# Delta rule exponents as matmul sums, triangular inverses from 16x16 blocks, and two buffer moves

## The chip, the cores and the metric

One NeuronCore of one Trainium2 chip runs the whole program. The metric is the device time of one execution in microseconds, the median of several runs; lower is better. TensorE (PE), VectorE (DVE), ScalarE (ACT), GpSimd (POOL) and the DMA queues (SP and POOL issue) work side by side and meet at semaphores.

## The reference, cut to what matters

A hybrid block (input projection, then Hyena, gated linear attention "GLA" and a gated delta rule "GDN" side by side, output projection, MLP) is followed by two layers of windowed attention with an mLSTM. The change touches the GDN and the attention:

```python
def gdn_chunk_scan(q, k, v, g, beta, s0):      # 4 heads of 96, two directions
        gcum = jnp.cumsum(gc, axis=-1)
        diff = gcum[..., :, None] - gcum[..., None, :]
        kb = kc * bc[..., None]
        a = -jnp.einsum('bhid,bhjd->bhij', kb, kc) * jnp.exp(jnp.where(strict, diff, -jnp.inf))
        rhs = jnp.concatenate([kb * jnp.exp(gcum)[..., None], vc * bc[..., None]], axis=-1)
        sol = lax.linalg.triangular_solve(eye - a, rhs, left_side=True, lower=True, unit_diagonal=True)
        ...
        attn = jnp.einsum('bhid,bhjd->bhij', qc, kc) * jnp.exp(jnp.where(incl, diff, -jnp.inf))
        o = (qc * jnp.exp(gcum)[..., None]) @ s + attn @ v_new
```

q and k are normalised per head (`l2norm`). In attention each block of 128 queries ends with `out / den`, times a gate.

## The kernel before, in words

All data are float32; large products use the fp32r form with a high and a low part (`mm3`: three matmuls). The kernel works in chunks of 128 tokens, 10 chunks (2 of context, 8 of the sequence), 4 heads and 2 directions, so 80 triangles of 128x128.

**Gates** (`gdn_gates`, `gdn_qrow`): rows of 40 (head, chunk) pairs by 128 tokens hold cumulated log decays G, logs of the write gate and of the norms (`gdn_lnorm`, which loads three partial sums into a small tile `gnsq`). The sums that the exponents need per column are stored to DRAM (`gdnRA`, `gdnRG`) and read back broadcast over 128 partitions (`bcast_row`, L1069).

**gdn_U** (L1073 to L1095): for each head and direction a broadcast row `ra` (128x1280) is loaded; for each of the 10 chunks one DVE scalar_tensor_tensor adds the column term `nG` and takes the minimum with a mask; one ACT exponential over 1280 columns; then k times k from TensorE is multiplied in, and the result U goes to DRAM (`gdnU`).

**gdn_inv** (L1097 to L1127): for each pair of heads, the 32x32 diagonal blocks of U (80 blocks per direction, one per partition) come back from DRAM and are inverted by 31 steps of a multiply (L1120) and an add (L1121) each; direction 0 on DVE, direction 1 on POOL. The inverses and their transposes (an ACT copy, `iU<-iE`) are stored as `gdnEd` and `gdnDd`.

**gdn_E** (L1129 to L1173), one call per head and direction: U, the diagonal blocks E and their transposes D0 are loaded; off-diagonal 32x32 and then 64x64 blocks are made with two small matmuls each, out of PSUM tiles that rotate through three banks (`px`). The caller `gdn_pre` (L1183) then makes W and G from E and stores them. Its second part has its own memory pool, opened after that of gdn_U and gdn_inv is closed; tiles E (one per direction), the rows and G have one buffer each.

**gdn_scan** (L1231, lanes from L1243): two lanes of two heads each. A head begins with loads, exponents (`rg` broadcast, eight DVE operations on `at`, ACT exponentials of `at` and `qs`), then ten serial steps.

Beside these, `hy_mix` (Hyena's transform in DVE, PE, POOL and DMA work) and the remaining input projections (`pm` matmuls) are written next to them in the program. **What sets the order:** a planner of the framework, which simulates times, orders every engine's queue; data, buffers and PSUM banks bound it. Only PE in `attention` has an order by hand (`manual_schedule`). DVE, ACT, POOL and the SP and POOL DMA queues execute in order.

**attention** (L2302, called at L2263): per block of 8 heads, scores, softmax and values; `finish` (L2374 on) copies 1/den into a tile `r` on POOL (L2383), transposes it on PE into a `po` bank, loads the gate `gz` (L2389), multiplies the two on DVE (L2390) and the product with y on POOL (L2391). `r` shares the one buffer of the tag `fr` with the rope and silu scratch of the projection units that fill PE (`units`, L2220 to L2231, recorded as L263 and L293). `gz` has two buffers.

Of the kernel before, what the change touches and what calls it, by code (L numbers as in the profile page):

```python
# [96 lines left out]
def pack_consts1():  # L97
    P = Packer()
    j, i = np.meshgrid(np.arange(128), np.arange(128), indexing="ij")
    for nm, ok in (("gF", j <= i), ("gB", j >= i), ("gFs", j < i), ("gBs", j > i)):  # L100
        P.add(nm, np.where(ok, -NEG, NEG))
    return P
# [59 lines left out]
class Builder:  # L162
# [83 lines left out]
    def ps(self, tag="px"):  # L246
        return self.pools[tag].tile([128, 512], F32, name=self.nm(tag), tag=tag)
# [729 lines left out]
    def gdn_lnorm(self, sq, out):  # L977

        nc, V = self.nc, self.nc.vector
        t = self.small([40, 3, 128], "gnsq", 1)  # L980
        for i in range(3):
            nc.sync.dma_start(out=t[:, i], in_=sq[i].rearrange("h (c t) -> (h c) t", t=128))
        V.tensor_add(out=out, in0=t[:, 0], in1=t[:, 1])
        V.tensor_add(out=out, in0=out, in1=t[:, 2])
        self.act(out, out, AF.Ln, bias=self.epsc[:40])
        self.ts(out, out, -0.5, ALU.mult)

    def gdn_qrow(self, gt, sq):

        nc = self.nc  # L990
        lq = self.small([40, 128], "gnlq", 1)
        self.gdn_lnorm(sq, lq)
        self.ts(lq, lq, math.log(96 ** -0.5), ALU.add)
        gt["rg"] = self.dram("gdnRG", [2, 40, 128])
        for d in range(2):
            self.nc.vector.tensor_add(out=gt["G"][:, d], in0=gt["G"][:, d], in1=lq)
            nc.gpsimd.dma_start(out=gt["rg"][d], in_=gt["G"][:, d])

    def gdn_gates(self, tl, gd, sk):


        nc, V = self.nc, self.nc.vector
        R = tl("ac", 2, (128, 10, 128))
        aa, bb, g, lb = (R[:40, 2 * i : 2 * i + 2, :] for i in range(4))
        G, lk = self.small([40, 2, 128], "gnG", 1), self.small([40, 128], "gnlk", 1)
        self.gdn_lnorm(sk, lk)
# [18 lines left out]
        out = {}  # L1025
        p = self.ps()
# [7 lines left out]
        p = self.ps()  # L1034
# [14 lines left out]
        ra = self.dram("gdnRA", [2, 40, 128])  # L1049
        for d in range(2):  # L1050
            nc.gpsimd.dma_start(out=ra[d], in_=lb[:, d, :])
# [15 lines left out]
        return dict(G=G, ra=ra, nG=nG, beta=beta, nbg=nbg, el=el, ek=ek)  # L1067

    def bcast_row(self, t, src, h, c0=0):  # L1069
        v = src[h * 10 + c0 : h * 10 + 10, :].rearrange("c t -> (c t)").unsqueeze(0).broadcast_to([t.shape[0], TT - c0 * 128])  # L1070
        self.nc.sync.dma_start(out=t, in_=v)
# [25 lines left out]
    def gdn_inv(self, hp, tl, Ud, Ed, Dd):  # L1097

        nc = self.nc
        UE = []  # L1100
        for d in range(2):
            U, E = tl(f"iU{d}", 2, (80, 32, 32)), tl(f"iE{d}", 2, (80, 32, 32))
            for hh in range(2):
                for b in range(4):
                    bs = slice(b * 32, b * 32 + 32)
                    p0 = hh * 40 + b * 10
                    nc.sync.dma_start(out=U[p0 : p0 + 10], in_=Ud[hp * 2 + hh, d, :, bs, bs])
            nc.gpsimd.memset(E, 0.0)
            nc.gpsimd.memset(E.rearrange("p a b -> p (a b)")[:, ::33], 1.0)
            UE.append((U, E))  # L1110
        for i in range(31):
            for d in range(2):
                eng = nc.gpsimd if d else nc.vector
                U, E = UE[d]
                m = i if d else 31 - i
                rows = slice(0, m) if d == 0 else slice(m + 1, 32)
                cols = slice(m, 32) if d == 0 else slice(0, m + 1)
                nr, ncl = rows.stop - rows.start, cols.stop - cols.start
                t = tl(f"it{d}", 1, (80, 272))[:, : nr * ncl].rearrange("p (a b) -> p a b", b=ncl)
                eng.tensor_mul(out=t, in0=U[:, rows, m : m + 1].broadcast_to([80, nr, ncl]), in1=E[:, m : m + 1, cols].broadcast_to([80, nr, ncl]))  # L1120
                eng.tensor_add(out=E[:, rows, cols], in0=E[:, rows, cols], in1=t)  # L1121
        for d in range(2):
            U, E = UE[d]
            self.act(U, E.rearrange("p a b -> p b a"), AF.Copy)
            for hh in range(2):
                nc.gpsimd.dma_start(out=Ed[hp * 2 + hh, d].rearrange("b c j i -> (b c) j i"), in_=E[hh * 40 : hh * 40 + 40])
                nc.gpsimd.dma_start(out=Dd[hp * 2 + hh, d].rearrange("b c j i -> (b c) j i"), in_=U[hh * 40 : hh * 40 + 40])  # L1127

    def gdn_E(self, h, d, tl, ps, Ud, Ed, Dd, E, D1):  # L1129

        nc, V = self.nc, self.nc.vector
# [7 lines left out]
        v32 = lambda p: p[:, :320].rearrange("p (c t) -> p c t", t=32)  # L1139
# [43 lines left out]
    def gdn_pre(self, dr, gt):  # L1183
# [3 lines left out]
        Ud, Ed, Dd = (self.dr_gdn[n] for n in ("U", "E", "D"))  # L1187
        with ExitStack() as es:
            tl = self.tiler(self.pool(es, "gdnp"))
            for hp in range(2):  # L1190
                for h in (2 * hp, 2 * hp + 1):
                    kT = tl("k", 1, (96, TT))
                    nc.sync.dma_start(out=kT, in_=dr["k"][h * 96 : h * 96 + 96])
                    self.gdn_U(h, kT, gt, tl, self.ps, Ud)
                self.gdn_inv(hp, tl, Ud, Ed, Dd)
        with ExitStack() as es:
# [3 lines left out]
            for t in Es + D1:  # L1200
                nc.gpsimd.memset(t, 0.0)
            for h in range(4):
# [6 lines left out]
                for d in range(2):  # L1209
# [5 lines left out]
                    self.gdn_E(h, d, tl, self.ps, Ud, Ed, Dd, E, D1[d])  # L1215
# [27 lines left out]
    def gdn_lane(self, tl, dr, gt, orows, heads):  # L1243
# [6 lines left out]
        for h in heads:  # L1250
# [432 lines left out]
    def block1(self, x3, ey):  # L1683
# [349 lines left out]
    def layer2(self, l, md, xT, ex, x_in, x_out):  # L2033
# [21 lines left out]
        with ed, ExitStack() as eu:  # L2055
# [157 lines left out]
            with self.psums(po=1, pm=1), ExitStack() as e2:  # L2213
# [49 lines left out]
                self.attention(lambda tag, *k: ol("fr", *k) if tag == "r" else al(tag, *k), pa, order, kA, kB, vr, qd, saz, yT, sink, nsink, step, more)  # L2263
# [38 lines left out]
    def attention(self, al, pa, tiles, kA, kB, vr, qd, saz, yT, sink, nsink, step, more):  # L2302
# [71 lines left out]
        def finish(b):  # L2374
# [7 lines left out]
            r = al("r", 1, (128, 8, 64))  # L2382
# [77 lines left out]
```

## Time and profile before

| | us |
|---|---|
| median of 3 runs | 3780.87 |
| the runs | 3768.03 to 3788.92 |
| the profiled execution | 3778.99 |
| its span, first to last instruction | 3777.2 |
| PE busy in it | 3311.5 |
| DVE busy | 2444.6 |
| mean granted TensorE clock | 0.903 of full speed |

Times of rows are counted from the span's start. "Busy" is the union of an engine's instructions; matmuls overlap each other, so a matmul's own duration is longer than its share of PE. The chain of waits is followed back from the last instruction, and so is one path, not all of them.

### The profile page before, as it was taken

Reading aid. Unit: us, or ns where it says so; the run is one execution under the profiler, and the core shown is the slowest. Engines: PE = TensorE matmul, PEld = TensorE weight load, DVE = VectorE, ACT = ScalarE, POOL = GpSimd, SP = SyncE. Lnnn points to the kernel's source line nnn. Section 1 sums busy time; section 2 is a strip of 40 time slices with the busy share of each in tenths; the row PEclk is TensorE's granted clock in tenths of the full one; section 3 lists DMA queues with packets and bytes.
Section 4 is the critical chain, followed back from the end, with each engine's and each line's share of the span. In section 5 each row is a group of like instructions: output and inputs, shape, how many; then the busy total and the mean of one; then the engine's idle time right before and its main releaser. Section 6 shows DMA issues by size and latency. Waiting matters only on the chain.

```text
span 3777.2 us, 50749 instructions
## 1 busy us (share of the span) xinstructions
PE 3311.5 (88%) x18398; PEld 2757.2 (73%) x18398; DVE 2444.6 (65%) x4678; ACT 1553.7 (41%) x2979; POOL 1436.9 (38%) x1250
## 2 busy tenths in 40 slices
PE   6899869866787999999999799998699999998897
PEld 5568647755676777887788588887588778876785
DVE  8797772789666465555644757665567656665676
ACT  4453236433233342222212444443455554453662
POOL 3234695563555344333312201112535511113454
PEclk9799989677657899999999799999899999999998
DMA  7545627865413453222221111113424421124343
GB/s 257 179 143 176 170 65 191 269 193 160 120 51 120 168 174 92 76 84 78 75 81 45 62 50 55 50 55 100 143 87 134 151 64 58 54 69 131 109 134 134
DMA packets 363077, 435.22 MB, mean 115 GB/s; under 512 B 68891, under 2 KB 284163, under 8 KB 362828
## 3 DMA queue, kind: packets, MB, share of 16 engines
q1 hardware_dynamic: 335596, 334.35, 30.2%
q0 software_dynamic: 27232, 97.63, 7.1%
q8 instruction: 146, 2.39, 0.3%
q14 instruction: 103, 0.84, 0.1%
HBM read 330.09 MB, written 101.81 MB: 114 GB/s over the span
## 4 chain that ended last, share of the span: by engine, by line
PE 52%; DVE 16%; DMA 7%; issue 5%; ACT 5%; POOL 5%; SPq 0%; POOLq 0%; DVEq 0%; ACTq 0%
PE pm L251 30%; PE px L251 16%; PE pa L251 2%; PE px L260 1%; POOL iE L1121 1%; PE po L251 1%; PE pa L260 1%; DMA mr<-in_w_ada 1%; DVE ma L266 1%; DVE at L266 1%; ACT e L263 1%; DMA wr<-in_w_in 1%; POOL ma L386 1%; DVE wl L282 1%; DMA st<-gdnRG 1%
## 5 line engine op out<-in xcount | busy, mean ns | idle before, releaser
L251 PE MATMUL pm<-x,wh 128*128 128x512 f32 (+3 forms) x4768 | 1429.5, 381 | 1.8 <-DVE x L282 1.8
L251 PEld LDWEIGHTS pm<-x,wh 128*128 128x128 f32 (+2 forms) x4768 | 870.6, 190 | 166.5 <-issue 7.1
L251 PE MATMUL pm<-x,wl 128*128 128x512 f32 (+3 forms) x2384 | 912.7, 383 | 29.3 <-ACT u L263 18.1
L251 PEld LDWEIGHTS pm<-x,wl 128*128 128x128 f32 (+2 forms) x2384 | 454.3, 191 | 116.6 <-ACT u L263 20.5
L251 PE MATMUL pm<-wo,ch 128*128 128x512 f32 x832 | 273.6, 409 | 0.0
L282 DVE TENSOR_TENSOR wl<-wr,wh 128x1024 fp32r<-128x1024 f32 (+1 forms) x110 | 148.4, 1349 | 151.9 <-ACT wh L263 151.7
L1626 DVE TENSOR_TENSOR oa<-px,oa 128x512 f32<-128x512 f32 x240 | 161.7, 688 | 129.7 <-PE px L251 129.6
L386 POOL TENSOR_TENSOR ma<-ma,mr 128x1024 f32<-128x1024 f32 x63 | 160.1, 2542 | 172.1 <-ACT mr L263 152.0
L263 ACT ACTIVATE u<-pm 128x512 f32<-128x512 f32 (+2 forms) x204 | 108.3, 544 | 269.1 <-PE pm L251 236.3
L251 PE MATMUL px<-w2h,ml 128*128 128x512 f32 x480 | 194.6, 405 | 21.1 <-DVE ml L282 17.5
L251 PE MATMUL px<-w2h,mh 128*128 128x512 f32 x480 | 192.8, 402 | 0.0
L251 PE MATMUL px<-w2l,mh 128*128 128x512 f32 x480 | 192.1, 400 | 0.0
L251 PEld LDWEIGHTS pm<-wo,ch 128*128 128x128 f32 x832 | 163.9, 198 | 33.8 <-issue 0.4
L270 POOL TENSOR_SCALAR mkw<-kr,gws 128x128 f32<-128x128 f32 x144 | 80.6, 564 | 282.1 <-PE px L251 238.9
L251 PE MATMUL pm<-wo,cl 128*128 128x512 f32 x416 | 174.0, 418 | 7.2 <-POOL cl L282 6.2
L2344 DVE TENSOR_REDUCE amx<-pa 128x1 f32<-128x640 f32 (+2 forms) x144 | 107.5, 746 | 78.4 <-PE pa L251 77.3
L263 ACT ACTIVATE e<-e 128x1280 f32<-128x1280 f32 (+3 forms) x126 | 134.2, 1068 | 45.5 <-DVE e L270 42.5
L263 ACT ACTIVATE wh<-wr 128x1024 fp32r<-128x1024 f32 (+2 forms) x138 | 143.3, 1038 | 19.7 <-PE pm L251 12.5
L263 ACT ACTIVATE P<-pa,amx 128x640 f32<-128x640 f32 (+2 forms) x144 | 105.6, 734 | 104.0 <-DVE amx L270 90.4
L263 ACT ACTIVATE w2h<-wr 128x1024 fp32r<-128x1024 f32 x32 | 33.9, 1059 | 264.5 <-PE px L251 226.5
L1524 POOL TENSOR_TENSOR xr<-or,xr 128x512 f32<-128x512 f32 x72 | 93.8, 1303 | 105.0 <-DVE or L1523 89.6
L263 ACT ACTIVATE mr<-mr,silu_cc 128x1024 f32<-128x1024 f32 x63 | 72.3, 1148 | 141.8 <-DVE ma L266 127.0
(879 smaller groups left out, 7442.3 us busy)
## 6 DMA issues: line engine op xcount, KB each, us to landing
wr<-in_w_in SPq DMA_DIRECT2D x102, 512.0 KB
wr<-in_w_mlp SPq DMA_DIRECT2D x64, 512.0 KB
mr<-in_w_ada SPq DMA_DIRECT2D x48, 512.0 KB
TF<-dft SPq DMA_DIRECT2D x54, 384.0 KB
mr<-in_w_mod SPq DMA_DIRECT2D x32, 512.0 KB
xp<-xr POOLq DMA_DIRECT2D x26, 512.0 KB, 3.9
xr<-xp SPq DMA_DIRECT2D x26, 512.0 KB
wr<-in_w_out SPq DMA_DIRECT2D x24, 512.0 KB
```

The source lines that it names most:

```text
L251: self.nc.tensor.matmul(out, a, b, start=start, stop=stop)
L260: self.nc.tensor.transpose(out, in_, self.ident[:p, :p])
L263: self.nc.scalar.activation(out, in_, f, **kw)
L266: self.nc.vector.scalar_tensor_tensor(out=out, in0=in0, scalar=scalar, in1=in1, op0=op0, op1=op1)
L270: (eng or self.nc.vector).tensor_scalar(out=out, in0=in0, scalar1=s1, scalar2=s2, op0=op0, **kw)
L282: (leng or self.nc.vector).tensor_sub(out=lo, in0=src, in1=hi.bitcast(F32))
L386: nc.gpsimd.tensor_add(out=acc[v], in0=acc[v], in1=raw)
L1121: eng.tensor_add(out=E[:, rows, cols], in0=E[:, rows, cols], in1=t)
L1524: nc.gpsimd.tensor_add(out=xr[:, fs], in0=r, in1=xr[:, fs])
L1626: V.tensor_add(out=oa[t][:, fs], in0=p, in1=oa[t][:, fs])
L2344: V.reduce_max(m_, s[:, w0:768], axis=AX.X)
```

## The change

Exponents: the masks with -inf, a selector and the row and column terms become fp32r operands (high part in partitions 0 to 39, low part in 64 to 103), and TensorE adds mask, column term and row term into one PSUM bank, from which ACT takes the exponential. The loads of `ra` and `rg` and the DVE additions go. Inverses: DVE and POOL invert 16x16 blocks for both heads of a pair in one instruction (15 steps in place of 31); gdn_E makes the 32x32 inverses with two more products, and their transposes with DVE. Partial sums of norms land in a part of a tile `ac` (for k) or a smaller `gnsq`. In attention `r` is taken from the tag of `gz`.

```diff
+    def gdn_hilo(self, name, src):
+        t = self.small([128, 128], name, 1, F32R)
+        self.nc.gpsimd.memset(t.bitcast(F32), 0.0)
+        self.act(t[0:40], src, AF.Copy)
+        self.nc.vector.tensor_sub(out=t[64:104], in0=src, in1=t[0:40].bitcast(F32))
+        return t
...
+    def gdn_decay(self, p, gt, row, d, h, c0, n, mask):
+        pv, hc = p[:, : n * 128].rearrange("p (c t) -> p c t", t=128), h * 10 + c0
+        self.mm(pv, self.identR, mask[:, d * 128 : d * 128 + 128].unsqueeze(1).broadcast_to([128, n, 128]), True, False)
+        self.mm(pv, gt["ng"][d], self.gm[:, 256 + hc : 256 + hc + n].unsqueeze(2).broadcast_to([128, n, 128]), False, False)
+        for i in range(n):
+            self.gdn_row(pv[:, i], gt[row][d], hc + i, False, i == n - 1)
+
+    def gdn_row(self, p, row, hc, first, last):
+        self.mm(p, self.gm[:, 256 + hc : 257 + hc].broadcast_to([128, p.shape[0]]), row, first, last)
...
     def gdn_U(self, h, kT, gt, tl, ps, Ud):
-        for d in range(2):
-            ra, U = tl("ra", 2, (128, TT)), tl("U", 2, (128, 10, 128))
-            self.bcast_row(ra, gt["ra"][d], h)
-            for c in range(10):
-                col = d * 40 + h * 10 + c
-                self.stt(U[:, c], ra[:, c * 128 : c * 128 + 128], gt["nG"][:, col : col + 1], self.k["gFs" if d == 0 else "gBs"], ALU.add, ALU.min)
-            self.act(U, U, AF.Exp)
...
         for c0 in range(0, 10, 4):
             n = min(4, 10 - c0)
+            for d, U in enumerate(Us):
+                p = ps()
+                self.gdn_decay(p, gt, "ra", d, h, c0, n, self.gm)
+                self.act(U[:, c0 : c0 + n], C3(p, n), AF.Exp)
...
-    def gdn_inv(self, hp, tl, Ud, Ed, Dd):
+    def gdn_inv(self, hp, tl, Ud, Ed):
...
-            U, E = tl(f"iU{d}", 2, (80, 32, 32)), tl(f"iE{d}", 2, (80, 32, 32))
+            U, E = tl(f"iU{d}", 2, (80, 2, 16, 16)), tl(f"iE{d}", 2, (80, 2, 16, 16))
             for hh in range(2):
-                for b in range(4):
...
+                for b in range(8):
+                    bs = slice(b * 16, b * 16 + 16)
+                    nc.sync.dma_start(out=U[b * 10 : b * 10 + 10, hh], in_=Ud[hp * 2 + hh, d, :, bs, bs])
...
-        for i in range(31):
+        for i in range(15):
...
-            self.act(U, E.rearrange("p a b -> p b a"), AF.Copy)
...
-    def gdn_E(self, h, d, tl, ps, Ud, Ed, Dd, E, D1):
+    def gdn_E(self, h, d, tl, ps, Ud, Ed, E, D1, Ec):
...
+        for b in range(8):
+            nc.sync.dma_start(out=Ec[b * 16 : b * 16 + 16, :, b % 2 * 16 : b % 2 * 16 + 16], in_=Ed[h, d, b].rearrange("c j i -> j c i"))
+        D16, Zc, E32, D0 = (tl(n, 2, (128, 10, 32)) for n in ("D0", "Z", "Z", "D0"))
+        V.transpose(flat(D16), flat(Ec))
+        pz, pe = v32(ps()), v32(ps())
+        for c in range(10):
+            for b in range(4):
+                self.mm(pz[blk(b), c], U[blk(b), c, blk(b)], D16[blk(b), c])
+        V.tensor_mul(out=Zc, in0=pz, in1=self.k["dF" if d == 0 else "dB"].unsqueeze(1).broadcast_to([128, 10, 32]))
+        for c in range(10):
+            for b in range(4):
+                self.mm(pe[blk(b), c], Zc[blk(b), c], Ec[blk(b), c])
+        V.tensor_add(out=E32, in0=pe, in1=Ec)
+        V.transpose(flat(D0), flat(E32))
         for b in range(4):
-            nc.sync.dma_start(out=E[blk(b), :, blk(b)], in_=Ed[h, d, b].rearrange("c j i -> j c i"))
-            nc.sync.dma_start(out=D0[blk(b)], in_=Dd[h, d, b].rearrange("c j i -> j c i"))
+            self.act(E[blk(b), :, blk(b)], E32[blk(b)], AF.Copy)
...
-                rg, a = tl("st", 2, (128, T)), tl("at", 4, (128, 8, 128))
-                self.bcast_row(rg, gt["rg"][d], h, 2)
-                for c in range(8):
...
-                self.act(a, a, AF.Exp)
-                q = tl("qs", 4, (96, T))
-                self.act(q, rg[:96], AF.Exp)
+                a, q = tl("at", 4, (128, 8, 128)), tl("qs", 4, (96, T))
+                for c0 in (0, 4):
+                    p = ps()
+                    self.gdn_decay(p, gt, "rg", d, h, 2 + c0, 4, self.wmask)
+                    self.act(a[:, c0 : c0 + 4], C3(p), AF.Exp)
+                    p = ps()
+                    for i in range(4):
+                        self.gdn_row(p[:96, i * 128 : i * 128 + 128], gt["rg"][d], h * 10 + 2 + c0 + i, True, True)
+                    self.act(q[:, c0 * 128 : c0 * 128 + 512], p[:96], AF.Exp)
...
-                self.attention(lambda tag, *k: ol("fr", *k) if tag == "r" else al(tag, *k), pa, order, kA, kB, vr, qd, saz, yT, sink, nsink, step, more)
+                self.attention(al, pa, order, kA, kB, vr, qd, saz, yT, sink, nsink, step, more)
...
-            r = al("r", 1, (128, 8, 64))
+            r = al("gz", 2, (128, 8, 64))
```

## Rows read from the trace of the kernel before

**Rows 1.** The page's head and its first part: span, PE busy (share) xinstructions.
```profile
span 3777.2 us, 50749 instructions
...
PE 3311.5 (88%) x18398; PEld 2757.2 (73%) x18398; DVE 2444.6 (65%) x4678; ACT 1553.7 (41%) x2979; POOL 1436.9 (38%) x1250
```
**Rows 2.** The page's fourth part, chain that ended last, by line.
```profile
PE pm L251 30%; PE px L251 16%; PE pa L251 2%; PE px L260 1%; POOL iE L1121 1%; PE po L251 1%; PE pa L260 1%; DMA mr<-in_w_ada 1%; DVE ma L266 1%; DVE at L266 1%; ACT e L263 1%; DMA wr<-in_w_in 1%; POOL ma L386 1%; DVE wl L282 1%; DMA st<-gdnRG 1%
```
**Rows 3.** Windows: length, busy PE, PEld, DVE, ACT, POOL; clock, DMA share, GB/s.
```profile
350.00:478.00 128.00, 112.90 (x545) 94.36 (x544) 90.31 (x182) 32.08 (x41) 72.71 (x93) 0.93 0.65 179
478.00:575.00 97.00, 65.43 (x266) 47.63 (x264) 65.61 (x102) 34.38 (x41) 86.98 (x90) 0.84 0.28 80
...
670.00:811.00 141.00, 116.21 (x1189) 107.56 (x1189) 111.23 (x142) 72.00 (x127) 79.02 (x44) 0.74 0.76 239
811.00:1000.00 189.00, 109.80 (x615) 99.19 (x615) 156.78 (x297) 51.06 (x86) 83.27 (x43) 0.66 0.56 166
1000.00:1150.00 150.00, 123.62 (x1043) 105.83 (x1044) 110.70 (x202) 54.44 (x143) 90.42 (x62) 0.57 0.20 54
```
**Rows 4.** Chain of waits, 350 to 575 us, shares by line.
```profile
by line: POOL iE L1121 21.3%; DMA gdnU<-U 8.8%; POOL it L1120 8.5%; DVE U L266 7.9%; issue 7.0%; DVE it L1120 5.2%; DVE iE L1121 4.7%; DVE wl L282 3.6%; DVE ac L266 3.4%; PE pm L251 3.3%; ACT iU L263 1.9%; DMA wr<-in_w_in 1.8%; SPq L1107 1.
```
**Rows 5.** Timelines of POOL, DVE and PE, 485 to 540 us: start, length, what, [idle before].
```profile
485.12 0.35 POOL L1121 TENSOR_TENSOR iE<-iE,it 80x87 f32<-80x87 f32 x1
...
495.61 23.36 POOL L1121 TENSOR_TENSOR iE<-iE,it 80x207 f32<-80x207 f32 x1
...
518.09 0.42 DVE L1121 TENSOR_TENSOR iE<-iE,it 80x255 f32<-80x255 f32 x1
...
536.89 3.58 PE L251 MATMUL px<-e,cols 128*4 128x512 f32 x4 [22.16 <-ACT e L263]
```
**Rows 6.** Windows of the inverse's tile iE alone: length, busy DVE, ACT, POOL.
```profile
350.00:478.00 128.00, 29.93 (x56) 1.62 (x1) 55.30 (x73) 0.93 0.65 179
478.00:575.00 97.00, 32.74 (x68) 6.88 (x4) 69.81 (x68) 0.84 0.28 80
```
**Rows 7.** Groups of DVE and ACT, 340 to 1110 us: busy us, mean ns | idle before.
```profile
L266 DVE SCALAR_TENSOR_TENSOR at<-st,gnnG,consts 128x128 f32<-128x128 f32 x64 | 44.0, 753 | 12.3 <-DMA st<-gdnRG 12.3
L266 DVE SCALAR_TENSOR_TENSOR U<-ra,gnnG,consts 128x128 f32<-128x128 f32 x80 | 25.3, 389 | 18.0 <-DMA gdnU<-U 10.8 <-issue 7.2
...
L1155 DVE COPY E<-px 32x320 f32<-32x320 f32 x16 | 7.8, 486 | 19.3 <-PE px L251 19.0
...
L263 ACT ACTIVATE iU<-iE 80x1024 f32<-80x1024 f32 x4 | 8.5, 2125 | 27.6 <-POOL iE L1121 22.7 <-DVE iE L1121 4.8
...
L263 ACT ACTIVATE D<-D 32x320 f32<-32x320 f32 x16 | 7.5, 468 | 9.9 <-DMA D<-gdnDd 9.5
```
**Rows 8.** Timelines of PE and ACT in gdn_E.
```profile
593.70 1.35 PE L251 MATMUL px<-D,U 32*32 32x32 f32 x40
...
676.63 0.57 ACT L263 ACTIVATE W<-px 128x480 f32<-128x480 f32 x1 [2.86 <-issue]
...
802.62 0.57 ACT L263 ACTIVATE W<-px 128x480 f32<-128x480 f32 x1 [4.10 <-PE px L251]
```
**Rows 9.** Groups of PE, 575 to 1110 us.
```profile
L251 PE MATMUL px<-E,nk 128*96 128x128 f32 x160 | 22.2, 291 | 0.7 <-ACT W L263 0.7
```
**Rows 10.** Timeline of PE: two first matmuls of a triple, one triple apart.
```profile
505.73 0.39 PE L251 MATMUL pm<-x,wl 128*128 128x512 f32 x1
...
506.41 0.39 PE L251 MATMUL pm<-x,wl 128*128 128x512 f32 x1
```
**Rows 11.** Chain of waits, 620 to 1110 us, shares by line.
```profile
by line: PE px L251 31.1%; DVE at L266 6.6%; issue 5.4%; DMA st<-gdnRG 4.3%; PE pm L251 3.8%; DVE EO L266 3.6%; DVE fl L282 2.5%; DVE Y L518 2.1%; DMA hx<-hy 1.8%; DVE P L266 1.7%; DVE S L266 1.7%; DMA G<-gdn_GT 1.6%; DVE b L820 1.6%; DVE l
```
**Rows 12.** Group of PE in attention; timeline of DVE around 2770 us.
```profile
L260 PE MATMUL po<-consts,fr 128*128 128x128 f32 x72 | 13.0, 311 | 40.5 <-POOL fr L2383 37.5 <-DVE y L2371 2.2 <-POOL wo L282 0.8
...
2757.97 0.20 DVE L2381 RECIPROCAL arden<-arden 128x8 f32<-128x8 f32 x1
...
2770.17 0.69 DVE L293 TENSOR_TENSOR or<-or,fr 128x512 f32<-128x512 f32 x1 [1.80 <-ACT fr L263]
```

More of the change, by code (lines that the diff above doesn't have):

```diff
@@ L99, in pack_consts1 @@
     j, i = np.meshgrid(np.arange(128), np.arange(128), indexing="ij")
-    for nm, ok in (("gF", j <= i), ("gB", j >= i), ("gFs", j < i), ("gBs", j > i)):
-        P.add(nm, np.where(ok, -NEG, NEG))
+    for nm, ok in (("sF", j < i), ("sB", j > i)):
+        P.add(nm, np.where(ok, 0.0, NEG))
+    p, q = np.meshgrid(np.arange(128), np.arange(40), indexing="ij")
+    P.add("sel", (p % 64 == q).astype(np.float32))
+    p, q = np.meshgrid(np.arange(128) % 32, np.arange(32), indexing="ij")
+    P.add("dF", ((p >= 16) & (q < 16)).astype(np.float32))
+    P.add("dB", ((p < 16) & (q >= 16)).astype(np.float32))
     return P
@@ L974, in head_norm_out, with gdn_lnorm @@
                 nc.gpsimd.dma_start(out=rows(yT, row0), in_=gt)
-    def gdn_lnorm(self, sq, out):
+    def gdn_lnorm(self, sq, out, t):
         nc, V = self.nc, self.nc.vector
[L980 to L984, printed above, removed]
+        for i, o in enumerate((t[:, 0], t[:, 1], out)):
+            nc.sync.dma_start(out=o, in_=sq[i].rearrange("h (c t) -> (h c) t", t=128))
+        V.tensor_add(out=t[:, 0], in0=t[:, 0], in1=t[:, 1])
+        V.tensor_add(out=out, in0=out, in1=t[:, 0])
         self.act(out, out, AF.Ln, bias=self.epsc[:40])
         self.ts(out, out, -0.5, ALU.mult)
+    def gdn_hilo(self, name, src):
[4 more added lines that the diff above has]
+        return t
     def gdn_qrow(self, gt, sq):
-        nc = self.nc
         lq = self.small([40, 128], "gnlq", 1)
-        self.gdn_lnorm(sq, lq)
+        self.gdn_lnorm(sq, lq, self.small([40, 2, 128], "gnsq", 1))
         self.ts(lq, lq, math.log(96 ** -0.5), ALU.add)
-        gt["rg"] = self.dram("gdnRG", [2, 40, 128])
+        gt["rg"] = []
         for d in range(2):
             self.nc.vector.tensor_add(out=gt["G"][:, d], in0=gt["G"][:, d], in1=lq)
-            nc.gpsimd.dma_start(out=gt["rg"][d], in_=gt["G"][:, d])
+            gt["rg"].append(self.gdn_hilo(f"gnra{d}", gt["G"][:, d]))
+    def gdn_decay(self, p, gt, row, d, h, c0, n, mask):
[6 more added lines that the diff above has]
+        self.mm(p, self.gm[:, 256 + hc : 257 + hc].broadcast_to([128, p.shape[0]]), row, first, last)
     def gdn_gates(self, tl, gd, sk):
@@ L1048, in gdn_gates @@
         V.tensor_add(out=lb, in0=lb, in1=lk.unsqueeze(1).broadcast_to([40, 2, 128]))
-        ra = self.dram("gdnRA", [2, 40, 128])
-        for d in range(2):
-            nc.gpsimd.dma_start(out=ra[d], in_=lb[:, d, :])
+        V.tensor_sub(out=g, in0=lk.unsqueeze(1).broadcast_to([40, 2, 128]), in1=G)
+        ra, ng = ([self.gdn_hilo(f"gn{n}{d}", t[:, d]) for d in range(2)] for n, t in (("ra", lb), ("ng", g)))
         p = self.ps()
@@ L1066, in gdn_gates @@
         self.stt(nbg, nbg, -1.0, beta, ALU.mult, ALU.mult)
[L1067 to L1071, printed above, removed]
+        return dict(G=G, ra=ra, ng=ng, beta=beta, nbg=nbg, el=el, ek=ek)
     def gdn_U(self, h, kT, gt, tl, ps, Ud):
         nc = self.nc
-        kk = []
-        Us = []
-        for d in range(2):
-            ra, U = tl("ra", 2, (128, TT)), tl("U", 2, (128, 10, 128))
-            self.bcast_row(ra, gt["ra"][d], h)
-            for c in range(10):
-                col = d * 40 + h * 10 + c
-                self.stt(U[:, c], ra[:, c * 128 : c * 128 + 128], gt["nG"][:, col : col + 1], self.k["gFs" if d == 0 else "gBs"], ALU.add, ALU.min)
-            self.act(U, U, AF.Exp)
-            Us.append(U)
+        Us = [tl("U", 2, (128, 10, 128)) for _ in range(2)]
+        C3 = lambda p, n: p[:, : n * 128].rearrange("p (c t) -> p c t", t=128)
         for c0 in range(0, 10, 4):
             n = min(4, 10 - c0)
+            for d, U in enumerate(Us):
+                p = ps()
+                self.gdn_decay(p, gt, "ra", d, h, c0, n, self.gm)
+                self.act(U[:, c0 : c0 + n], C3(p, n), AF.Exp)
             p = ps()
@@ L1114, in gdn_inv @@
                 U, E = UE[d]
[L1115 to L1117 removed]
+                m = i if d else 15 - i
+                rows = slice(0, m) if d == 0 else slice(m + 1, 16)
+                cols = slice(m, 16) if d == 0 else slice(0, m + 1)
                 nr, ncl = rows.stop - rows.start, cols.stop - cols.start
[L1119 removed]
@@ L1120, in gdn_inv @@
-                eng.tensor_mul(out=t, in0=U[:, rows, m : m + 1].broadcast_to([80, nr, ncl]), in1=E[:, m : m + 1, cols].broadcast_to([80, nr, ncl]))
-                eng.tensor_add(out=E[:, rows, cols], in0=E[:, rows, cols], in1=t)
+                t = tl(f"it{d}", 1, (80, 2, 72))[:, :, : nr * ncl].rearrange("p h (a b) -> p h a b", b=ncl)
+                shape = [80, 2, nr, ncl]
+                eng.tensor_mul(out=t, in0=U[:, :, rows, m : m + 1].broadcast_to(shape), in1=E[:, :, m : m + 1, cols].broadcast_to(shape))
@@ L1122, in gdn_inv @@
+                eng.tensor_add(out=E[:, :, rows, cols], in0=E[:, :, rows, cols], in1=t)
         for d in range(2):
-            U, E = UE[d]
-            self.act(U, E.rearrange("p a b -> p b a"), AF.Copy)
             for hh in range(2):
-                nc.gpsimd.dma_start(out=Ed[hp * 2 + hh, d].rearrange("b c j i -> (b c) j i"), in_=E[hh * 40 : hh * 40 + 40])
-                nc.gpsimd.dma_start(out=Dd[hp * 2 + hh, d].rearrange("b c j i -> (b c) j i"), in_=U[hh * 40 : hh * 40 + 40])
-    def gdn_E(self, h, d, tl, ps, Ud, Ed, Dd, E, D1):
+                nc.gpsimd.dma_start(out=Ed[hp * 2 + hh, d].rearrange("b c j i -> (b c) j i"), in_=UE[d][1][:, hh])
@@ L1186, in gdn_pre @@
         nc = self.nc
-        Ud, Ed, Dd = (self.dr_gdn[n] for n in ("U", "E", "D"))
+        Ud, Ed = (self.dr_gdn[n] for n in ("U", "E"))
         with ExitStack() as es:
@@ L1194, in gdn_pre @@
                     self.gdn_U(h, kT, gt, tl, self.ps, Ud)
-                self.gdn_inv(hp, tl, Ud, Ed, Dd)
+                self.gdn_inv(hp, tl, Ud, Ed)
         with ExitStack() as es:
@@ L1199, in gdn_pre @@
             D1 = [tl("D1", 2, (128, 10, 64)) for _ in range(2)]
-            for t in Es + D1:
+            Ec = [tl("Ec", 2, (128, 10, 32)) for _ in range(2)]
+            for t in Es + D1 + Ec:
                 nc.gpsimd.memset(t, 0.0)
@@ L1214, in gdn_pre @@
                     nc.gpsimd.tensor_mul(out=W, in0=rows[1], in1=f("beta"))
-                    self.gdn_E(h, d, tl, self.ps, Ud, Ed, Dd, E, D1[d])
+                    self.gdn_E(h, d, tl, self.ps, Ud, Ed, E, D1[d], Ec[d])
                     G = tl("G", 1, (96, 10, 128))
@@ L1703, in block1 @@
             self.load_consts(kp, "consts1")
+            self.gm = kp.tile([128, 296], F32R, name="gm", tag="gm", bufs=1)
+            o = self.offs["consts1"][0]
+            for c0, nm in ((0, "sF"), (128, "sB"), (256, "sel")):
+                V.tensor_copy(out=self.gm[:, c0 : c0 + o[nm][1]], in_=self.k[nm])
             egg = ExitStack()
```

19 lines of the change are left out of this document (7 added, 12 removed).

## The prediction

> **What bounds the kernel now.** The page's head first: PE is busy 3311.5 of 3777.2 us, so 466 us at most are to be had without making its work less [rows 1]. The chain of the whole page gives PE nearly half, but lines of this change stand on it too: POOL's inverse step, DVE's `at`, the DMA that brings `st` from `gdnRG` [rows 2]. Since a mean over 3777 us hides stages, I cut windows around the Delta rule. Between 350 and 575 us PE is busy 112.9 + 65.4 of 225 us, so 47 us are idle there; from 670 to 1150 its clock is 0.74, 0.66 and 0.57, against 0.93 before 478 [rows 3] and 0.903 for the whole program. This stretch waits on chains, not on an engine that is full. The rest of the program is PE's and the change hardly touches it, attention apart.
>
> The execution shown took 3778.99 us, 1.9 below the median of 3780.87. The sum below is made against 3779. About 0.5% (19 us) is what a measurement here can tell from no change: faster means under 3762, slower over 3800.
>
> **Part 1: gdn_U and gdn_inv, 350 to 575.** The chain of these 225 us gives POOL `iE` 21.3%, `it` 8.5, DVE `it` 5.2 and `iE` 4.7, ACT `iU` 1.9: 41.6%, 94 us in the inverse [rows 4]. On `iE` alone POOL is busy 55.3 + 69.8 = 125.1 us, DVE 62.7, ACT 8.5 [rows 6]. One of POOL's steps lasts 23.36 us where one half its size lasts 0.35, and ends 0.5 us after the last of DVE's inverse steps; it lay beside DVE's whole run [rows 5]. The cost follows the number of steps and the overlap with DVE more than the elements. 62 multiply and add steps per pair of heads and direction become 30, for both pairs 124 become 60, with about half the elements each. POOL: 60 x 0.35 = 21 us in place of 125; DVE: 60 x 0.28 (a little over half of 62.7/124) = 17 in place of 62.7; ACT's 8.5 us go. The second pair's inverse, which held 478 to 573, should end near 490, and gdn_E with its own pool opens there: 87 us earlier for this line of work. DVE also loses 25.3 us of additions for U with the 18.0 us that they waited [rows 7].
>
> That is not 87 us of program: between 478 and 575 PE does projections that must be done anyhow. They gain what PE idles, 47 us at most. And the change adds PE work: per head and direction of gdn_U two sums over the first and second four chunks and a short third, 32 matmuls of 512 columns at 227 ns (a triple takes 0.68 us [rows 10]) plus 16 of 256 at half that, 9.2 us, and 80 row matmuls of 128 columns at about 139 ns by the nearest group [rows 9], 11 us: 20 (14 to 24, by 60 to 190 ns for a row matmul). 47 - 20 - 7 for what stays idle gives **20 us** for the projections. On SP, `iU` takes 64 small loads in place of 32 and `Ec` 64 in place of the 64 of E and D; 16 broadcasts go. All are queued ahead of gdn_E's loads only; covered while projections fill PE, some 14 us if that cover goes.
>
> A rule on the 23-us step: the Trainium skill ("SBUF — State Buffer", section "Who interferes with whom") says that a DVE instruction with two SBUF inputs contends with a GpSimd read, and that whoever comes first blocks the other for its whole instruction. By that rule a block lasts one DVE instruction, so the 23 us would have another cause, which fewer steps need not remove, and the sum would be that of rival 5 below, 3744, not 3722. The row shows a stall over a whole run of DVE steps, which the page does not state.
>
> **Part 2: gdn_E, 577 to 811.** Five steps (head, direction) of W evacuation lie between 676.63 and 802.62: 25.2 us a step [rows 8]. They run in series because three `px` banks rotate in program order, so the next step's first product waits for the evacuation of the previous step's G. A step gains, on that series: 40 matmuls of 32x32 (1.35 us [rows 8]), DVE's masking (0.5, like its 32x320 copy at 486 ns [rows 7]), 40 more (1.35), an addition (0.5), a transpose (0.5), four ACT copies (4 x 468 ns [rows 7] = 1.9): 6.1 us. From above: PE at half clock +2.7, and each of three DVE visits queues behind Hyena's work, DVE being busy 111 of 141 us [rows 3], about 1.3 us each: 13 us. From below: 0, if the step overlaps its neighbour, for E and D loads cost 9.5 us of ACT's waiting before [rows 7] and become one load that can be early. I take 9, nearer to the rows that name the operations: 8 x 9 = **+72** (0 to +104) for this line.
>
> **Part 3: gdn_scan.** DVE's 64 additions are 44.0 us [rows 7], and on the chain from 620 to 1110 (490 us) `at` holds 6.6%, the DMA from `gdnRG` 4.3%: 32 + 21 = 53 us [rows 11]. In their place PE forms 16 sums: 32 matmuls of 512 columns at 227 ns, 7.3, and 128 row matmuls at 139 ns, 17.8 (60 to 190 ns: 15 to 32 in all); ACT takes 32 exponentials of 512 columns from PSUM in place of 16 long ones over as many elements, 18 us by the 0.57 us of W's 480-column evacuation [rows 8], and so no more than before. Of this I put 33 us on the path at this clock: **-20**.
>
> **How the parts meet.** Two lines end near 1100. The Delta rule's own: -87 + 72 - 20 = -35. Hyena's and the projections': -20 from PE's idle time, and DVE, busy 156.8 of 189 us from 811 to 1000 [rows 3], loses about 100 us over the stretch (25.3 + 44.0 + 45.7, less 8 x 1.9 added); chain shares of DVE's Hyena lines `EO`, `fl`, `Y` are 8.2% of 490 = 40 us [rows 11], of which I take 15: -35. Both lines say **-35**, and the later one decides.
>
> **Part 4: attention.** Before the 72 transposes of 1/den PE idles 40.5 us, 37.5 of it behind POOL's copy into `fr` [rows 12]. In the case I followed, den was ready at 2758.2, but `fr` was held by silu scratch until 2770.9, when DVE's product ended [rows 12]. With the tag of `gz` this hold goes; r then sits in one of its two buffers and gz always in the other, so gz's load waits for POOL's product of the block before, a block earlier, which leaves it time. What remains is POOL's own queue (weight splits written ahead). I take 0.6 of 37.5: **-22** (0 to -37).
>
> Edits at no cost: high/low splits, the moved `gnsq`, and the copies to `gm` run on 40 to 128 short partitions while PE is full of projections; without that cover a few us.
>
> **Sum:** 3779 - 35 - 22 = **3722**.
>
> **Rivals.**
> 1. *The clock comes back.* On PE's 31.1% of the chain, 152 us of `px` work [rows 11] run at a mean of 0.66 [rows 3]. PE gets some 45 us of new work and fewer gaps; at 0.80 those 152 us become 125: -27. With two thirds of attention's remainder (-10): **3685**. For: the clock falls just where PE waits most. Against: the serial step gets longer, not denser. The Trainium skill ("TensorE: Matmul & The Clock Gate", Part 1) has it that the throttle is released by activity, which speaks for this rival; that 350 to 478, with PE busy 88%, has 0.93 agrees.
> 2. *r stays late.* POOL's splits and not `fr` held four of five copies: attention gives 0, the rest as forecast: **3744**.
> 3. *Hidden anyway.* Hyena's DVE line decides both ends and the projections only shift: the stretch gives 0, attention a few us: **3775**. For: DVE 156.8 of 189 us. It is also where the time would be if the planner's new order gave nothing earlier. That the change does not do what it says (sums wrongly hidden behind old waits, say) ends here too.
> 4. *Slower: gdn_E's round trips.* The new products put four more visits of DVE and ACT between PE's, and each step is serial. ACT stood still 2.86 and 4.10 us ahead of W [rows 8]; if every new visit costs 3.5 us behind Hyena's queue beside the 6.1 of work, a step grows by 20 us, 160 in all. The Delta rule's line: -87 + 160 - 20 = +53, less attention 22: **3810**. It decides from 16 us a step on, (87 + 20 + 22) / 8. For: DVE is busy 111 of 141 us there. Against: its waits are shared with the projections' and Hyena's, which go on meanwhile.
>
> 5. *POOL's long step comes back.* One POOL step of 23 us stands once more beside DVE's run, in the second pair, whatever the number of steps: 22 of the 87 us are not had, the Delta rule's line gives -87 + 22 + 72 - 20 = -13 in place of -35: **3744**. Against: DVE's run, which it outlasted by 0.5 us [rows 5], falls to about a quarter. This is the case that the page on SBUF leaves open.
>
> **Numbers.** Forecast 0.42; rival 1 0.17; rival 2 0.08; rival 3 0.15; rival 4 0.13; rival 5 0.05. Forecast, 1, 2 and 5 are under 3762: faster 0.72; rival 3 same 0.15; rival 4 slower 0.13. The forecast's own range is 3690 to 3755 (gdn_E's step between 6 and 11 us, attention 0 to -37). The whole range, 3660 to 3800, takes in rivals 1 to 3 and 5 with their bounds and leaves out most of rival 4 and a few hundredths below.
>
> **What would show it.** Right: POOL's last inverse step near 490 and none over 5 us; the first E product near 500; W evacuations 33 to 36 us apart; no `at` on DVE and no `gdnRG` on the chain; idle before the `po` transposes under 18 us. Wrong: the steps of gdn_E over 41 us apart (rival 4); a clock over 0.75 from 811 to 1150 (rival 1); PE still behind L2383's copy for over 30 us (rival 2); the last scan step near 1100 as now with DVE busy over 80% before it (rival 3).

## The result, and the profile after

The changed kernel took 3727.65 us (median of 4 runs) against 3777.36 before (4 runs): 49.7 us less, ratio 0.9868, 95% interval 0.983 to 0.9906. The forecast was 3722. The total came out; where it came from did not. The profiled execution's span is 3722.1 us. The head of the page and the windows that answer to [rows 1, 3], then one window of the first attention layer:

```profile
span 3722.1 us, 53759 instructions
...
PE 3350.3 (90%) x19966; PEld 2797.4 (75%) x19966; DVE 2339.3 (63%) x4512; ACT 1563.9 (42%) x3045; POOL 1350.8 (36%) x1182
```

```profile
350.00:478.00 128.00, 126.99 (x680) 108.24 (x678) 58.62 (x108) 37.02 (x63) 44.76 (x83) 1.00 0.51 137
478.00:575.00 97.00, 93.36 (x839) 72.31 (x838) 49.83 (x56) 47.82 (x73) 40.74 (x45) 0.98 0.50 136
670.00:811.00 141.00, 99.90 (x1339) 89.48 (x1340) 104.90 (x142) 68.20 (x120) 82.76 (x41) 0.71 0.65 203
811.00:1000.00 189.00, 144.87 (x1182) 131.55 (x1181) 127.78 (x246) 59.99 (x121) 78.14 (x43) 0.73 0.44 124
1000.00:1150.00 150.00, 133.22 (x1165) 115.82 (x1164) 83.72 (x202) 54.09 (x142) 72.79 (x49) 0.61 0.19 51
...
2700.00:2800.00 100.00, 95.98 (x617) 85.13 (x616) 73.32 (x134) 70.14 (x138) 50.39 (x43) 1.00 0.42 122
```

The first two lines look like a success: PE is busy 220 of 225 us where it was busy 178, at a granted clock of 1.00 and 0.98. Whether that is time won is seen only from where the stages end. Three lines of instructions mark them: W's evacuations in gdn_E (first and last start), the scan's products with `at`, and those of `v` in the gated linear attention (GLA), which runs after Hyena and beside the scan. Before:

```profile
L263 ACT ACTIVATE W<-px x16: 550/572/573, 624.6 to 807.6; 128x480 f32<-128x480 f32 x16
...
L251 PE MATMUL px<-W,at x128: 275/421/526, 873.8 to 1096.8; 128*128 128x96 f32 x128
...
L251 PE MATMUL px<-v,at x64: 245/421/529, 1056.5 to 1270.1; 128*128 128x96 f32 x64
```

After:

```profile
L268 ACT ACTIVATE W<-px x16: 548/571/572, 552.0 to 854.9; 128x480 f32<-128x480 f32 x16
...
L256 PE MATMUL px<-W,at x128: 275/386/527, 900.0 to 1131.9; 128*128 128x96 f32 x128
...
L256 PE MATMUL px<-v,at x64: 248/421/529, 1039.6 to 1268.9; 128*128 128x96 f32 x64
```

gdn_E starts 72.6 us earlier and ends 47.3 later, for it takes 303 us in place of 183 (from the first of these evacuations to the last). The scan ends 35 us later, and the linear attention, with which this stretch closes, at the same place (1.2 us earlier). PE's busy time from 350 to 1300, first before, then after:

```profile
sum 950.00, PE 747.61 PEld 632.52 DVE 623.93 ACT 340.57 POOL 531.45; mean PE 149.52 PEld 126.50 DVE 124.79 ACT 68.11 POOL 106.29
```

```profile
sum 950.00, PE 801.86 PEld 685.88 DVE 529.76 ACT 354.42 POOL 448.89; mean PE 160.37 PEld 137.18 DVE 105.95 ACT 70.88 POOL 89.78
```

PE is busy 54 us more and the stretch ends at the same place, so the idle time that the change removed went to the work that it added. DVE's 94 and POOL's 83 us less bought nothing that shows at the end. The gain stands in attention; the group of the transposes of 1/den that answers to [rows 12], and then, in the timelines of DVE and POOL, one block's reciprocal and copy:

```profile
L265 PE MATMUL po<-consts,gz 128*128 128x128 f32 x72 | 10.9, 274 | 4.0 <-DVE y L2403 4.0
```

```profile
2727.40 0.20 DVE L2413 RECIPROCAL arden<-arden 128x8 f32<-128x8 f32 x1
...
2727.74 0.61 POOL L2415 COPY gz<-arden 128x512 f32<-128x512 f32 x1 [0.46 <-DVE arden L2413]
```

The copy comes 0.14 us behind the end of the reciprocal, and the 37.5 us of waiting are gone.

### The profile page after: what moved, and what is told of

It reads as the page before. It is cut to its first block, busy times and chain, and to the rows that moved or that the text cites. A ratio compares the mean times of both kernels' runs of the same rounds, so it can differ in the third digit from the quotient of the medians.

```text
span 3722.1 us, 53759 instructions
## 1 busy us (share of the span) xinstructions
PE 3350.3 (90%) x19966; PEld 2797.4 (75%) x19966; DVE 2339.3 (63%) x4512; ACT 1563.9 (42%) x3045; POOL 1350.8 (36%) x1182
## 4 chain that ended last, share of the span: by engine, by line
PE 47%; DVE 10%; issue 5%; DMA 4%; ACT 4%; POOL 3%; SPq 0%; POOLq 0%; ACTq 0%; DVEq 0%
PE pm L256 28%; PE px L256 13%; PE pa L256 2%; PE po L256 1%; PE px L265 1%; PE pa L265 1%; DMA mr<-in_w_ada 1%; DVE ma L271 1%; ACT e L268 1%; DVE amx L2376 1%; DVE e L287 1%; DVE x L287 1%; DMA wr<-qd 1%; POOL ma L391 0%; POOL cl L287 0%
```

## Experiments

**Each part alone.** The theory after the traces (A): r's place is the whole gain. The rival (B): the prediction's sum.

attn_only:

```diff
-self.attention(lambda tag, *k: ol("fr", *k) if tag == "r" else al(tag, *k), pa, ...
+self.attention(al, pa, ...
...
-            r = al("r", 1, (128, 8, 64))
+            r = al("gz", 2, (128, 8, 64))
```

> Only the last two edits (r takes the tag of gz), the Delta rule as before. Theory A (r's place is the whole gain, because every late copy of r delayed the whole block of attention and not only its transposes): 45 to 53 us faster, about 3728. Theory B (the prediction's sum: 22 from attention, 35 from the Delta rule): about 3755. PE's idle time before the po transposes goes from 37.5 us to about 0 in both.

no_attn undoes these two lines in the changed kernel.

> The whole change but r left in the scratch fr. Theory A: within 8 us of the kernel before, 3770 to 3780, with the Delta rule's scan still ending some 35 us later than before. Theory B: about 3742.

exp_only takes gdn_hilo, gdn_decay, gdn_row and their callers; gdn_inv, gdn_E and attention stay as before.

> Only the exponents summed by TensorE (and the move of the norms' scratch); inverses of 32x32 and r as before. Theory A, with gdn_E's longer steps named as what ate the gain: the Delta rule's scan ends 10 to 40 us earlier than before, the program 0 to 15 us faster, since the linear attention that ends the stretch is not on that chain. Theory B: 20 to 30 us faster.

inv_only takes gdn_inv, gdn_E and Ec alone.

> Only the 16x16 inverses. Theory A: gdn_E starts 60 to 80 us earlier, its eight steps take 36 to 44 us each in place of 25, the scan ends 20 to 50 us later; the program from 5 us faster to 15 us slower. Theory B: 87 earlier and 72 longer, 10 to 20 us faster. If POOL's long step comes back (rival 5), one POOL inverse step of over 10 us stands in the trace.

inv_attn is inv_only with the edit of attn_only.

> The 16x16 inverses and r's place, without the exponents by TensorE. By the sum of the runs of single parts (45 from attention, 6 from the inverses): 3728, as the whole change; the exponents then give nothing. If the exponents need the early inverses to pay (the whole change less this run): 3740 or more. If they only add PE work: 3715 or less, and this run beats both kernels.

| run | us | before, same chip | ratio, 95% interval |
|---|---|---|---|
| attn_only | 3734.74 | 3779.39 | 0.9885 (0.9862 to 0.9909) |
| no_attn | 3771.84 | 3779.39 | 0.9987 (0.9968 to 1.0006) |
| exp_only | 3786.65 | 3779.39 | 1.0025 (0.9999 to 1.005) |
| inv_only | 3773.82 | 3779.39 | 0.9989 (0.9968 to 1.0011) |
| inv_attn | 3722.66 | 3781.20 | 0.9859 (0.9829 to 0.989) |

The size in theory A holds: r's place gives 44.7 us, the rest 7.5 with an interval that takes in nothing. Its reason (that a late copy delayed the whole block) no run tried by itself. The exponents alone lean to slower, and without them the other two parts are as fast as the whole change: they give nothing that shows. The scan of exp_only ends nearly where it did (1100.3 against 1096.8), not 10 us earlier: that expectation missed. In inv_only it ends 25 us later with steps of 42 us, as expected, and POOL's longest step is 6.6 us. In no_attn it ends 28 us later, where 35 were expected.

**What held r.** r_dve changes the kernel before, r_own the changed one:

```diff
-            nc.gpsimd.tensor_copy(out=r, in_=den...)
+            V.tensor_copy(out=r, in_=den...)
...
-            r = al("gz", 2, (128, 8, 64))
+            r = al("r", 1, (128, 8, 64))
```

> The kernel before, with r copied by DVE and not by POOL, still into the scratch fr. If POOL's queue (weight splits written ahead) held r, this gives 20 us or more, 3755 or less. If the buffer fr held it, nothing: 3765 to 3790, and PE still waits 30 us or more ahead of the po transposes, now for DVE.

> The whole change, with r in a buffer of its own, so that gz keeps both of its buffers. If gz's lost buffer costs something it shows here as 5 us or more under the change; if gz's load is early enough with one, as the prediction has it, the program is within 8 us of the change, 3718 to 3735.

r_dve: 3768.08, ratio 0.998 (0.9964 to 0.9996). A block of DVE's timeline, and PE's group:

```profile
2726.26 0.69 DVE L293 TENSOR_TENSOR or<-or,fr 128x512 f32<-128x512 f32 x1 [1.36 <-ACT fr L263]
2726.99 0.43 DVE L2383 COPY fr<-arden 128x512 f32<-128x512 f32 x1
```

```profile
L260 PE MATMUL po<-consts,fr 128*128 128x128 f32 x72 | 13.4, 317 | 34.4 <-DVE fr L2383 31.8 <-DVE y L2371 2.0 <-DVE amx L270 0.6
```

On another engine the copy still follows the silu product that frees `fr`, by 0.04 us, though 1/den was ready at 2711.2 and DVE stood idle for 1.36 us ahead of the product; PE still waits 31.8. With buffers of its own (the change, r_own) the wait is gone: the buffer held r. By the medians r_dve was 11 us faster than the kernel before (by the ratio 8); PE's wait is 5.7 us shorter, which may be POOL's queue. r_own: 3729.45, ratio 0.9875 (0.9845 to 0.9905), as the change; gz's lost buffer costs nothing that shows.

**Why the Delta rule gave nothing that shows.** Five kernels change gdn_E's new work inside the whole change. e_none leaves out what joins the 16x16 inverses:

```diff
...
-        V.tensor_mul(out=Zc, in0=pz, in1=...)
...
-        V.tensor_add(out=E32, in0=pe, in1=Ec)
-        V.transpose(flat(D0), flat(E32))
+        E32, D0 = Ec, D16
```

> The whole change, but gdn_E leaves out what joins the 16x16 inverses into 32x32 ones: both products, the mask, the addition and the second transpose (the off-diagonal 16x16 blocks stay zero). Theory A1 (the stretched steps of gdn_E push the scan into the linear attention and slow that down, so they ate the gain): steps about 25 us apart, the scan ends 60 to 110 us earlier than with the change, the program 15 to 30 us faster than it, 3695 to 3710. Theory A2 (Hyena and the linear attention end this stretch whatever the Delta rule does): the scan ends as much earlier, the program within 8 us of the change, 3718 to 3735.

e_act:

```diff
+        self.act(Zc[:, :, q0 : q0 + 16], pz[:, :, q0 : q0 + 16], AF.Copy, scale=self.k["dF" if d == 0 else "dB"][:, q0 : q0 + 1])
...
+            self.mm(pe[blk(b)], self.ident[blk(b), blk(b)], Ec[blk(b)], True, False)
...
+            self.mm(pd[blk(b)], self.ident[blk(b), blk(b)], D16[blk(b)], True, False)
...
+                self.mm(pd[blk(b), c], Ec[blk(b), c], Zc[blk(b), c], False, c == 9)
...
+        self.act(D0, pd, AF.Copy)
```

> The whole change, with the new visits of DVE in gdn_E replaced: ACT masks by a scale per partition, PE adds the diagonal blocks by an identity product and forms the transposes by products of its own, ACT evacuates. Only the first transpose stays on DVE. If DVE's queue behind Hyena's work is what stretches a step (theory A1): steps 28 to 33 us apart in place of 43, and the program 8 to 25 us faster than the change, 3703 to 3720. If the number of round trips stretches it, whichever engine serves them: 38 us or more and no gain.

e_dve:

```diff
-        V.tensor_mul(out=Zc, in0=pz, in1=...)
+        V.tensor_mul(out=Zc, in0=Ec, in1=...)
...
-        V.tensor_add(out=E32, in0=pe, in1=Ec)
+        V.tensor_add(out=E32, in0=Zc, in1=Ec)
```

> The whole change, with the two new products of gdn_E left out (the mask is applied to the 16x16 inverses themselves, and what comes of it is not the inverse), while the mask, the addition and the second transpose stay on DVE. It splits the 38 us by which the kernel without any of these beat the change. If the new visits in DVE's queue cost them: 3715 to 3735, as the change. If PE's two products and their round trips cost them: 3685 to 3700, as the kernel without. In between it splits by the number.

e_par has e_act's mask, `pd` as plain products, and

```diff
+        V.tensor_add(out=D0, in0=pd, in1=D16)
         V.tensor_add(out=E32, in0=pe, in1=Ec)
-        V.transpose(flat(D0), flat(E32))
```

> The whole change, computing the same with fewer visits in series: ACT masks by a scale per partition, the transposes come from 40 more small products on PE, and the two DVE additions stand side by side, so that DVE is on the series twice in place of four times. If DVE's visits cost the 38 us: 8 to 25 us faster than the change, 3703 to 3720. If PE's work does: the same or up to 15 us slower, 3725 to 3745.

e_thin:

```diff
-        for c in range(10):
+        for c in range(2):
...
+        V.tensor_mul(out=Zc[:, 2:], in0=Ec[:, 2:], in1=...)
...
+        V.tensor_add(out=E32[:, 2:], in0=Zc[:, 2:], in1=Ec[:, 2:])
```

> The whole change, with gdn_E's two new products made for two of the ten chunks only (16 small matmuls in place of 80 a step; the other eight chunks take the mask and the addition without a product, so that what comes of them is not the inverse). PE then has a fifth of the added work, but every step still goes from PE to DVE, back to PE and back to DVE. In the kernel without these products DVE's visits needed only the loads, so that run left the trips open. If PE's time for the products costs the 38 us: 3692 to 3702. If the trips between PE and DVE do: 3715 to 3735.

| run | us | ratio, 95% interval | W first to last |
|---|---|---|---|
| the change | 3727.65 | 0.9868 (0.983 to 0.9906) | 303 |
| e_none | 3689.94 | 0.9772 (0.9743 to 0.9802) | 238 |
| e_dve | 3691.48 | 0.977 (0.974 to 0.9799) | 227 |
| e_thin | 3694.91 | 0.9779 (0.9744 to 0.9813) | 262 |
| e_par | 3734.27 | 0.9879 (0.9849 to 0.9909) | 304 |
| e_act | 3772.83 | 0.9985 (0.9968 to 1.0002) | 353 |

The joining work does cost what the early inverses give: without it the program is 38 us faster. In e_none:

```profile
L268 ACT ACTIVATE W<-px x16: 549/571/573, 536.9 to 775.2; 128x480 f32<-128x480 f32 x16
...
L256 PE MATMUL px<-W,at x128: 275/276/529, 814.7 to 1050.9; 128*128 128x96 f32 x128
...
L256 PE MATMUL px<-v,at x64: 248/421/528, 1030.7 to 1243.2; 128*128 128x96 f32 x64
```

The linear attention ends 26 us earlier than with the change, its scan 81, so theory A2 (the stretch ends the same whatever the Delta rule does) falls; the steps were 34 us apart, not 25, and the time lay 5 us under the range of theory A1. So of the 120 us by which gdn_E grew, 55 stay with the joining work left out (238 against 183); whether the first transpose, the four copies or the earlier place among the projections makes them, no run separates. e_dve speaks against DVE's visits as such, for it keeps them (though there they wait only for loads); e_par too, but it also has PE make 40 more small products a step. e_thin keeps the trips and gives 33 of the 38 us. e_act falls in its second branch (a step took 50 us), but it doesn't tell trips from work: its identity products are dear (a group of 49 of 32x320 is busy 28.1 us from 575 to 1000).

Is it PE's time, then? The groups of PE, 500 to 900 us, of the changed kernel, of e_thin and of e_par (where `Ec,Zc` is the others' `Ec,Z`, and `Zc,Ec` the added product):

```profile
L256 PE MATMUL px<-D,U 32*32 32x32 f32 (+1 forms) x1120 | 40.6, 220 | 28.2 <-DVE D L1162 22.6 <-issue 3.6 <-ACT D L268 1.9
L256 PE MATMUL px<-Ec,Z 32*32 32x32 f32 x640 | 9.3, 215 | 20.5 <-DVE Z L1157 10.7 <-issue 6.5 <-ACT G L268 2.5
```

```profile
L256 PE MATMUL px<-D,U 32*32 32x32 f32 (+1 forms) x592 | 32.6, 224 | 11.6 <-ACT D L268 4.8 <-ACT G L268 2.1 <-DVE D L1165 2.0
L256 PE MATMUL px<-Ec,Z 32*32 32x32 f32 x128 | 3.2, 212 | 1.4 <-ACT G L268 0.8 <-DVE Z L1159 0.6
```

```profile
L256 PE MATMUL px<-D,U 32*32 32x32 f32 (+1 forms) x1040 | 38.6, 216 | 12.0 <-DVE D L1165 6.1 <-issue 3.8 <-ACT G L268 2.1
...
L256 PE MATMUL px<-Ec,Zc 32*32 32x32 f32 x640 | 9.7, 215 | 8.0 <-issue 8.0
L256 PE MATMUL px<-Zc,Ec 32*32 32x32 f32 x640 | 8.7, 208 | 3.5 <-ACT Zc L268 2.2 <-issue 1.3
```

e_thin saves 14 us of busy PE ((40.6 + 9.3) - (32.6 + 3.2)) and 31 of PE's waits for DVE's answers (22.6 + 10.7 against 2.0 + 0.6). The longest such wait in the changed kernel, on PE and on DVE:

```profile
659.01 1.60 PE L256 MATMUL px<-Ec,Z 32*32 32x32 f32 x80 [2.55 <-ACT G L268]
671.48 2.12 PE L256 MATMUL px<-D,U 32*32 32x32 f32 x40 [10.87 <-DVE D L1162]
```

```profile
664.00 0.69 DVE L522 TENSOR_TENSOR Y<-hx 128x512 f32<-128x512 f32 x1 [6.97 <-DMA hx<-hy]
...
669.16 0.48 DVE L1161 TENSOR_TENSOR Z<-px,Ec 128x320 f32<-128x320 f32 x1
...
670.83 0.50 DVE L1162 STREAM_TRANSPOSE D<-Z 128x320 f32<-128x320 f32 x1
```

The second products were done at 660.6 (659.01 + 1.60), but the addition stood in DVE's queue behind a Hyena instruction that waited for a DMA until 664, and behind four more of Hyena's until 669.16. Yet e_par took the waits for DVE's answers in these groups from 33.3 us to 6.1, and 2.2 for ACT's, and was not faster, with its added products (busy 8.7 us) on the other side. So the cost goes with the products; how it divides between their time on PE and the order that the planner, which orders each kernel anew, gives the queues around them stays open.

## Why the prediction was right in total and wrong in its parts

- **Attention** (forecast 22, bounds 0 to 37; measured 44.7 alone). The step that failed is "What remains is POOL's own queue (weight splits written ahead). I take 0.6 of 37.5". The followed case was the rule: r_dve shows `fr` behind 31.8 us of wait. The upper bound fell too by the medians: 44.7 here, 44.2 from no_attn to the change, 51.2 from inv_only to inv_attn, though the interval of the first alone (34 to 52) takes 37 in. That a stall costs more than its length is read from the clock. From 2700 to 2800 it was 0.86 before and is 1.00 now; the transposes right behind the three long stalls of the first layer lasted 1.12, 1.11 and 1.12 us, at a granted clock of 0.50 (1.2 GHz), and 0.60 to 0.63 now. The cost behind the stalls was not tried by itself. The window before and one of the three, then one of the transposes now:

```profile
2700.00:2800.00 100.00, 77.49 (x442) 68.36 (x441) 58.89 (x102) 54.09 (x110) 35.76 (x30) 0.86 0.29 84
...
2735.89 1.11 PE L260 MATMUL po<-consts,fr 128*128 128x128 f32 x4 [10.39 <-POOL fr L2383]
```

```profile
2763.74 0.60 PE L265 MATMUL po<-consts,gz 128*128 128x128 f32 x4
```

- **The inverses** went as forecast: POOL's multiply and add steps fell from 117 us to 30 (forecast 21), the last starts at 489.2 (forecast 490). gdn_E's first product came 91 us earlier (502.3 against 593.7; forecast 87), its first W evacuation 73. POOL's steps before, and now:

```profile
L1121 POOL TENSOR_TENSOR iE<-iE,it 80x31 f32<-80x31 f32 (+15 forms) x62 | 67.7, 1093 | 4.2
L1120 POOL TENSOR_TENSOR it<-iU,iE 80x31 f32<-80x31 f32 (+15 forms) x62 | 49.3, 795 | 18.2 <-DMA iU<-gdnU 14.0
```

```profile
L1134 POOL TENSOR_TENSOR it<-iU,iE 80x30 f32<-80x30 f32 (+7 forms) x30 | 15.1, 502 | 20.1 <-DMA iU<-gdnU 18.1
L1135 POOL TENSOR_TENSOR iE<-iE,it 80x30 f32<-80x30 f32 (+7 forms) x30 | 14.9, 497 | 2.2
```

  Rival 5 is out: POOL's longest step is 1.30 us. The long step stands in all four kernels that keep 32x32 inverses: 23.36 us [rows 5], 23.33 in attn_only, 22.52 in exp_only, 23.32 in r_dve. The prediction misread its company: of the 30 DVE instructions that start beside it only 13 are inverse steps, and DVE's inverse goes on at 538.73, so what it outlasts by 0.5 us is a gapless run of DVE and not the inverse. With the change POOL's last inverse step ends at 490.3, before the place where the long one began (493.9 to 495.6); whether fewer steps or only the earlier time spared it stays open.
- **gdn_E** (forecast +72, bounds 0 to 104; measured +120 between the first and the last evacuation, 303 - 183, and +139 from the first product on): 40.8 us a step between the two evacuations, five steps apart, that answer to [rows 8], about the sign set for rival 4:

```profile
648.62 0.57 ACT L268 ACTIVATE W<-px 128x480 f32<-128x480 f32 x1 [3.79 <-PE px L256]
...
852.70 0.57 ACT L268 ACTIVATE W<-px 128x480 f32<-128x480 f32 x1 [6.14 <-PE px L256]
```

  The step that failed is "From above: ... 13 us": it grew by 16. The term was sized by the operations' own durations. For the products these were about right: [rows 8] shows 20 of them (40 records), the new ones are 40, and 40 took 0.89 us at a clock of 1.00 and 1.60 at 0.59. The mechanism of rival 4, DVE's and ACT's new visits, is not what the runs bear out: with visits but no products (e_dve) the time is that of e_none.
- **The scan** gave 12 of 20 us: from W's last evacuation to its own end 277 us, before 289. So the Delta rule's line is -73 + 120 - 12 = +35, which is what the scan's end shows.
- **"Both lines say -35, and the later one decides"** failed twice: the Delta rule's came to +35, and the other does not end with Hyena. The linear attention follows it, and starts 17 us earlier (1039.6 against 1056.5) but runs beside a later scan, and ends where it did. How long it lasts goes with how long the scan runs beside it: from its first product with `v` and `at` to its last it took 203 to 215 us in the six traces in which the two share 20 to 47 us (the kernel before among them, 214), and 223 to 236 in the eight in which they share 89 to 100 (the change: 229). e_none starts it 9 us earlier than the change and shares 20, and ends it at 1243.2; e_thin starts it 35 us earlier, shares 98, and ends it at 1236.6. That the scan slows it is read from these, not tried by itself.
- **Rivals and signs.** Rival 3 was right for the stretch's size, not for attention. Rival 1: the clock from 811 to 1150 rose from 0.66 and 0.57 to 0.73 and 0.61, under its sign of 0.75. Rival 2 fell with attn_only. Of the signs of being right, POOL's last step, gdn_E's first product and the idle time before the transposes (4.0 us) came true; the 33 to 36 us between evacuations did not.
- **Price of PE's work:** 54 us more from 350 to 1300, by the windows, against some 67 forecast.

Two errors, 23 us in attention and 28 in the Delta rule, of opposite sign, gave a total within 6 us: that it came out is luck. The total alone would have taught the wrong lesson.

## What to carry to other kernels

Judge an edit by where its stage ends, not by the engine time that it frees: 94 us of DVE and 83 of POOL were free here and nothing that shows came of them. A scratch buffer shared between a serial chain and filling work can stop the chain at every turn; look for it when a copy starts only behind the last reader of its buffer, however early its input was ready. When a change joins a buffer move with rewritten arithmetic, time them apart: two lines carried this one.

## What was not expected of the hardware

One POOL instruction lasts 23 us while DVE runs instructions without a gap, and the place hardly moves: 495.61 us in the kernel before and 495.63 in attn_only. In all four kernels that show it, it ends 0.4 to 0.5 us behind DVE's run; why is open.

In the kernel before, the four longest waits of PE ahead of the attention transposes (6.9 to 10.4 us) were each followed by transposes at a granted clock of 0.50, of 1.11 to 1.12 us.
